# Hybrid attention and SSD layer: V's DRAM copies, convolution tiles and split-weight stores issued by GpSimd, output weights split in 20 products, one pair more from raw weights

## The chip, the core and the metric

The kernel runs on one core of a Trainium2 chip. The core has five engines that run side by side, each through its own list of instructions in order: TensorE (PE; its weight loads are shown as PEld), VectorE (DVE), ScalarE (ACT), GpSimd (POOL) and SyncE (SP), which only issues transfers (DMAs). ScalarE and GpSimd issue transfers too, from the same list as their arithmetic. The metric is the time of one execution in microseconds (us) on the device, the median of 3 runs; less is better.

## The reference

One decoder layer on x (2048 tokens, 1024 wide, float32). An input projection of 6672 columns feeds two branches, attention over three dilations and a Mamba-2 state-space mixer; both are gated and normed, joined and projected back. Cut to what matters here:

```python
proj = jnp.einsum('bsd,de->bse', x, w_in[layer])
q, k, v, z_att, z_ssm, xbc, dt_raw = jnp.split(proj, list(SPLITS), axis=-1)
o1, l1 = dilated_window_attention(q, k, v, slopes, 1)
o2, l2 = dilated_window_attention(q, k, v, slopes, 4)
o3, l3 = dilated_window_attention(q, k, v, slopes, 16)
wts = jax.nn.softmax(jnp.stack([l1, l2, l3], axis=0), axis=0)
y_att = wts[0][..., None] * o1 + wts[1][..., None] * o2 + wts[2][..., None] * o3
y_att = rms_norm(y_att.reshape(Bsz, S, D_ATT) * jax.nn.silu(z_att), att_norm_g[layer])
xbc = jax.nn.silu(causal_depthwise_conv(xbc, conv_w[layer], conv_b[layer]))
xs, bm, cm = jnp.split(xbc, [...], axis=-1)
...
y = ssd_chunked(xs_h, dt, a, bm, cm) + d_skip[layer][:, None] * xs_h
y_ssm = rms_norm(y.reshape(Bsz, S, D_SSM) * jax.nn.silu(z_ssm), ssm_norm_g[layer])
mix = jnp.concatenate([y_att, y_ssm], axis=-1)
out = jnp.einsum('bse,ed->bsd', mix, w_out[layer])
x = layer_norm(alpha * x + out, ln_g[layer], ln_b[layer])
```

## The kernel before

Every float32 operand of a large product is held as a high and a low part (h and l in the tile names), and a product is three matmuls: high x high, high x low, low x high.

**Stages.** (1) To 211 us: V and dt are projected; x is split, and parts and half-sums of x are stored to DRAM (d_T) for the next stage. The first eight row blocks of the output weights are scaled, split and stored to d_wo here (`split_w`). A scheduler orders this stage. (2) To 1279 us: 44 **jobs**, each of two 128-column blocks times one half of the tokens (1024). A job is a Strassen-like scheme of seven products in the order B11, T1, B21, T2, B22, T4, T3 (`products`); a product is 12 matmuls of 128 x 512. The token side of the half lies in 14 tiles (TB11h, TB11l, TT1h, ... of 128 x 2048, 1 MB each), loaded from d_T by GpSimd (L229, `token_side`) when the half changes: before job 0, during job 9 for job 10, during job 31 for job 32. The column side is four blocks of raw weights per job: ScalarE issues the loads `wr<-w` (L240) two jobs ahead, VectorE forms sums (L254), ScalarE casts the high part (L261), GpSimd subtracts for the low part (L262), giving seven tiles w. ScalarE (L315) or VectorE (L321, L323) moves each product out of PSUM, and TensorE needs the bank again three products later. (3) To about 1800 us: attention. (4) To the end: the output projection.

**Jobs.** Jobs 0 to 9 are the convolution ("c") and SSM gate ("s") columns of the first half; 10 to 31 the second half with all columns; 32 to 43 q, k and z of the first half. For jobs 32 to 43 the four weight tiles that are sums were saved to d_wc by SyncE when they were made for the second half (L264), and are reloaded by GpSimd (L282, `column_reload`); the other three are made anew from raw weights (L285, L286). From job 22 on the chunk steps of the state-space mixer (`ssd1` to `ssd6`) run between the products.

**What sets the order.** In stage 2 the order is written by hand: after each product `flush` runs what stands in `later` for this product's number (seven per job), and `after(n, f)` puts f n products later. So each engine's list is fixed, and a transfer waits in the list of the engine that issues it. Side work that hangs on the numbers:

- `copy_v`: 32 copies of V within DRAM, 512 KB each, in the two orders that the dilations 4 and 16 need, issued by ScalarE (L492), one every four products from product 3 on (jobs 0 to 18).
- `wout_load` and `split_w`: the other eight row blocks of the output weights, as 16 halves: load by ScalarE (L652), three products later the split by ScalarE (L117) and VectorE (L118), and at once the store by SyncE (L119); halves are loaded from product 36 to 61.
- `conv_tile`: the tile U of a convolution block, 128 x 19 x 128. Three transfers by SyncE (L391 twice in 512-byte rows, L392) bring the first half's results from d_cu, where job 0 to 9 put them (L385); the second half's products are added beside them, then ScalarE and VectorE run the four taps over U (L409, L412), ScalarE the SiLU (L418), and SyncE stores it (L424, L427). There are two U buffers.
- `sums_load`, `sums_part`: the half-sums of x; those of the first half are made in stage 1, those of the second in jobs 1 to 4 (L100, L108 to L112).
- SyncE also stores every finished column block (d_za, d_qh, ... L354, L365, L366, L377).

Of the kernel before, what the change touches and what calls it, by code (L numbers as in the profile page):

```python
# [9 lines left out]
F32 = mybir.dt.float32  # L10
# [7 lines left out]
D = 1024  # L18
# [10 lines left out]
def hybrid_layer(ctx, tc, xT, xc, w52, wv, convw, convb, dtb, alog, dskp, gcol, wout,  # L29
# [56 lines left out]
    with ExitStack() as c1:  # L86
# [25 lines left out]
            nc.sync.dma_start(dap(d_T[p, nm], k * 512, [[2048, 128], [128 * 2048, 2], [1, 512]]), t.bitcast(F32))  # L112


        def split_w(e, hf, raw, t):
            g = gc[:, e:e + 1]
            nc.scalar.activation(t[:, 0], raw, AF.Copy, scale=g)  # L117
            nc.vector.scalar_tensor_tensor(t[:, 1], raw, g, t[:, 0].bitcast(F32), op0=OP.mult, op1=OP.subtract)  # L118
            nc.sync.dma_start(d_wo[e][:, :, hf * 512:hf * 512 + 512], t.bitcast(F32))  # L119


        with tc.tile_pool(name="ts", bufs=1, reuse_waits="tile") as ts, \
# [57 lines left out]
            for pc in range(4):  # L180
                for i in range(2):
                    pst = [pp.tile([128, 512], F32, name="pp") for _ in range(5)]
                    pst += [ss.tile([128, 512], F32, name="ss") for _ in range(3)]
                    for k in range(8):
                        if i == 0:
                            load_v(pc, k)
                        if pc == 0:
                            load_x(k, i)
                        for r in range(8):
                            v_mm(pst[r], pc, 8 * i + r, k)  # L190
                    for r in range(8):
                        v_out(pst[r], pc, 8 * i + r)
                if pc == 0:
                    nc.sync.dma_start(ident, cst[:, 0:128])
                    nc.sync.dma_start(tri, cst[:, 128:256])
                    nc.sync.dma_start(cw, convw)
                    nc.sync.dma_start(cb, convb)
                    nc.sync.dma_start(dsk, dskp)
                    nc.sync.dma_start(gc, gcol)
                if pc < 2:  # L200
                    for k in (2 * pc, 2 * pc + 1):
                        r = sums_load(ts, 0, k)
                        for c in range(4):
                            sums_part(ts, 0, k, r, c)
                if pc in (1, 2):
                    quarters(pc - 1)
                if pc > 1:
                    for e in range(4 * pc - 8, 4 * pc - 4):
                        raw = ts.tile([128, 1024], F32, name="st", bufs=4)
                        nc.sync.dma_start(raw, wout[e * 128:(e + 1) * 128])  # L210
                        for hf in range(2):
                            split_w(e, hf, raw[:, 512 * hf:512 * hf + 512],
                                    ts.tile([128, 2, 512], F32R, name="to", bufs=6))
# [174 lines left out]
        def conv_tile(i, U):  # L388
            u = cp.tile([128, 19, NJ], F32, name="U", bufs=2)
            for tb in range(2):  # L390
                nc.sync.dma_start(u[:, 3 + tb:19:4, :], d_cu[i][:, tb].rearrange("p (s j) -> p s j", j=NJ))  # L391
            nc.sync.dma_start(u[:, 0, 1:NJ], d_cu[i][:, 1, 3 * NJ:4 * NJ - 1])  # L392
            nc.gpsimd.memset(u[:, 0:3, 0:1], 0.0)
            U.append(u)

# [93 lines left out]
        def copy_v(d, b):  # L489

            o = (b % 4 * 512 + b // 4 * 32, 8 * b)[d - 1]
            nc.scalar.dma_start(d_v[d][b], dap(d_v[0], o * D, [[128 * D, (4, 16)[d - 1]], [D, (32, 8)[d - 1]], [1, D]]))  # L492


        b64 = lambda a, n, g: a[:, n, 8 * g:8 * g + 8][:, :, None].to_broadcast([128, 8, 64])
# [150 lines left out]
        with tc.manual_schedule(engines={E.PE, E.DVE, E.Activation, E.Pool}):  # L646
# [3 lines left out]
            def wout_load(j):  # L650
                raw = sums.tile([128, 512], F32, name="woraw", bufs=3)
                nc.scalar.dma_start(raw, wout[j // 2 * 128:j // 2 * 128 + 128, j % 2 * 512:j % 2 * 512 + 512])  # L652
                after(3, lambda: split_w(j // 2, j % 2, raw, sums.tile([128, 2, 512], F32R, name="wot", bufs=4)))
            for j in range(16):
                later.setdefault(7 * 5 + 1 + 5 * j // 3, []).append(lambda j=j: wout_load(16 + j))
            for j in range(32):
                later.setdefault(4 * j + 3, []).append(lambda j=j: copy_v(1 + j // 16, j % 16))
            sums = sub.enter_context(tc.tile_pool(name="sums", bufs=1, side="right", reuse_waits="tile"))
            raws = {0: sums_load(sums, 1, 0)}
            for m, (ph, (kind, i)) in enumerate(jobs):  # L660
                p = ph % 2
                nT = T
                if m + 1 < len(jobs):
                    ph2 = jobs[m + 1][0]
                    if ph2 == 2:
                        nW, prep = column_reload(m + 1 - 32, q)
                    else:
                        u = [x for _, x in jobs[32:]].index(jobs[m + 1][1]) if jobs[m + 1][1] in rest else None
                        nW, prep = column_side(q, u)
                    for j, f in enumerate(prep):  # L670
                        after(j, f)
# [2 lines left out]
                        for j in range(7):  # L674
                            after(j, steps[j])
                if m + 2 < len(jobs):
                    q2, steps_ = column_load(*cts[m + 2], nc.scalar, jobs[m + 2][0] == 2)
                    for n, f in zip((3, 4, 6, 7), steps_):
                        after(n, f)
                if 10 < m + 1 < len(jobs) and jobs[m + 1][1][0] == "c":  # L680
                    Un = [None]
                    after(5, lambda i=jobs[m + 1][1][1], U=Un: (U.clear(), conv_tile(i, U)))
                to = None
                if kind == "c" and p == 0:
                    fin = fin_u(i)
                elif kind == "c":
                    U, U2 = U2 or [], None
                    if not U:
                        after(0, lambda i=i, U=U: conv_tile(i, U))
                    after(3, lambda i=i, U=U: conv_tile(i + 1, U))  # L690
                    to = lambda ci, q, U=U: U[ci][:, 5 + q:19:4, :]
                    fin = conv_fin(i, U)
                elif kind == "s":
# [552 lines left out]
```

## Time and profile before

| | us |
|---|---|
| median of 3 runs | 2204.65 (2201.44 to 2204.94) |
| profiled execution | 2207.89 |
| its span, first to last instruction | 2206.1 |
| TensorE busy in it | 2058.6 (93%) |
| ScalarE, VectorE, GpSimd busy | 1153.3, 1375.1, 1047.0 |

| stretch | length us | TensorE busy us | mean DMA share |
|---|---|---|---|
| V projection, 0 to 211.2 | 211.2 | 191.6 | 0.96 |
| jobs 0 to 22, 211.2 to 725.5 | 514.3 | 464.4 | 0.75 |
| jobs with chunk steps, to 1279 | 553.5 | 525.2 | 0.88 |
| attention, to 1800 | 521.0 | 507.3 | 0.70 |
| output, to 2206.1 | 406.1 | 370.1 | 0.39 |

How to read it: the profile is one execution. Busy time counts arithmetic; an engine that waits to issue a transfer counts as idle. In the lists of waits and in timelines, `<-` behind an idle time names what ended it, an instruction or the landing of a transfer (`DMA out<-in`). ACTq and SPq are the issuing of transfers by ScalarE and SyncE. Some matmul records can be missing from a trace.

### The profile page before, as it was taken

To read this page: it belongs to the slowest core of one execution; us is meant where nothing else is said; L and a number is where in the kernel's file an instruction comes from. 1 tells how busy PE (TensorE), PEld (TensorE's weight loads), DVE (VectorE), ACT (ScalarE), POOL (GpSimd) and SP (SyncE) were. 2 spreads that over 40 slices of the span, in tenths; PEclk is the share of its full clock that TensorE was granted. 3 is DMA by queue.
4 is the path that set the end of the run, shared out by engine and by line. 5 is a ranking of instruction groups with operands and counts; after the bars stand their busy time and mean duration, and the time that the engine had idled before them with its cause. 6 is when DMAs were issued, how large, how long until landed. Compare 5 with 4: busy or idle time off the path is not lost.

```text
span 2206.1 us, 38841 instructions
## 1 busy us (share of the span) xinstructions
PE 2058.6 (93%) x13824; PEld 1712.9 (78%) x13824; DVE 1375.1 (62%) x3141; ACT 1153.3 (52%) x3003; POOL 1047.0 (47%) x815
## 2 busy tenths in 40 slices
PE   8999899869999999979999999999999986999998
PEld 7998777648887787857888878888788865888886
DVE  3431554328899677735555548888888855655655
ACT  3231444326555676645666558888888841222221
POOL 2123434436776576744555422766666671322322
PEclk9999989979999999989999979999999988999999
DMA  9999677886767888898889853778777799332220
GB/s 328 370 327 337 219 264 243 298 327 183 243 208 265 306 308 305 299 400 276 283 263 291 279 208 115 218 220 241 222 195 207 209 366 271 107 107 83 86 90 29
DMA packets 275377, 529.19 MB, mean 240 GB/s; under 512 B 44784, under 2 KB 136048, under 8 KB 259184
## 3 DMA queue, kind: packets, MB, share of 16 engines
q1 hardware_dynamic: 201312, 272.93, 38.9%
q0 software_dynamic: 29968, 154.15, 19.6%
q10 hardware_dynamic: 43904, 99.64, 13.7%
q8 instruction: 109, 1.79, 0.3%
q14 instruction: 84, 0.69, 0.1%
HBM read 347.98 MB, written 195.43 MB: 246 GB/s over the span
## 4 chain that ended last, share of the span: by engine, by line
PE 49%; DMA 14%; DVE 7%; ACT 5%; issue 4%; POOL 3%; ACTq 1%; SPq 0%; DVEq 0%; POOLq 0%
PE N L861 6%; PE S L812 6%; PE T L841 6%; PE pp L306 5%; PE pp L310 5%; PE pp L308 5%; PE S L1021 3%; PE S L1023 3%; PE S L1022 3%; PE T L1021 2%; PE T L1022 2%; PE T L1023 2%; DVE acc L412 2%; DMA U<-d_cu 2%; DMA zt<-d_zs 2%
## 5 line engine op out<-in xcount | busy, mean ns | idle before, releaser
L262 POOL TENSOR_TENSOR w<-wr,w 128x512 fp32r<-128x512 f32 x224 | 357.0, 1614 | 226.3 <-ACT w L261 192.8
L828 ACT ACTIVATE P<-P,st 128x256 f32<-128x256 f32 (+1 forms) x768 | 345.2, 451 | 98.0 <-DVE st L820 97.5
L820 DVE CUSTOM_DVE_ANT_0 P<-S,tb 128x256 f32<-128x256 f32 (+1 forms) x768 | 235.1, 362 | 83.7 <-PE S L812 46.3
L315 ACT COPY ev<-pp 128x512 f32<-128x512 f32 x176 | 102.3, 581 | 208.1 <-PE pp L310 121.0
L843 DVE COPY PT<-T 128x512 f32<-128x512 f32 (+1 forms) x304 | 196.5, 677 | 1.4 <-PE T L841 1.4
L841 PE MATMUL T<-ident,P 128*128 128x128 f32 x1200 | 178.8, 286 | 5.9 <-DVE PT L843 5.9
L861 PE MATMUL N<-PT,v 128*64 128x128 f32 x2400 | 176.4, 284 | 1.0 <-DMA v<-d_v 1.0
L261 ACT CAST w<-wr 128x512 fp32r<-128x512 f32 x224 | 133.7, 618 | 75.8 <-DVE wr L254 36.7
L254 DVE TENSOR_TENSOR wr<-wr 128x512 f32<-128x512 f32 x128 | 129.2, 1010 | 66.6 <-DMA wr<-w 62.4
L861 PEld LDWEIGHTS N<-PT,v 128*64 128x64 f32 x2400 | 129.2, 138 | 34.2 <-issue 22.6
L841 PEld LDWEIGHTS T<-ident,P 128*128 128x128 f32 x1200 | 129.8, 142 | 30.2 <-DVE PT L843 7.2
L828 ACT ACTIVATION_READ_ACCUMULATOR P<-P,st 128x1 f32 x768 | 143.8, 187 | 0.0
L928 POOL TENSOR_TENSOR wb<-num,wb 128x2048 f32<-128x2048 f32 x21 | 96.3, 4588 | 98.5 <-ACT P L828 71.1
L323 DVE TENSOR_TENSOR ev<-pp,ev 128x512 f32<-128x512 f32 x152 | 100.6, 682 | 51.8 <-PE pp L310 39.6
L812 PE MATMUL S<-kh,qp 64*128 64x256 f32 (+1 forms) x1024 | 126.5, 306 | 0.0
L998 DVE TENSOR_REDUCE tb<-P 128x128 f32<-128x1024 f32 x32 | 63.9, 1998 | 84.4 <-PE N L1027 49.2
L363 DVE SCALAR_TENSOR_TENSOR ev<-ev 128x512 f32<-128x512 f32 x64 | 66.6, 1054 | 64.1 <-ACT ev L362 64.0
L812 PEld LDWEIGHTS S<-kh,qp 64*128 64x128 f32 x1024 | 88.9, 188 | 22.0 <-issue 20.7
L146 PE MATMUL pp<-vh,xh 128*128 128x256 f32 (+1 forms) x320 | 90.4, 289 | 15.8 <-ACT xh L169 15.8
L412 DVE SCALAR_TENSOR_TENSOR acc<-U,cw,acc 128x2048 f32<-128x2048 f32 x36 | 101.3, 2813 | 3.1 <-ACT acc L409 2.6
L139 POOL TENSOR_TENSOR vl<-vraw,vh 128x256 fp32r<-128x256 f32 (+1 forms) x32 | 30.0, 940 | 131.7 <-ACT vh L138 110.0
L147 PE MATMUL pp<-vl,xh 128*128 128x256 f32 (+1 forms) x320 | 90.8, 288 | 0.0
(364 smaller groups left out, 6037.3 us busy)
## 6 DMA issues: line engine op xcount, KB each, us to landing
wr<-w ACTq DMA_DIRECT2D x156, 256.0 KB
d_wc<-w SPq DMA_DIRECT2D x48, 512.0 KB
w<-d_wc POOLq DMA_DIRECT2D x48, 512.0 KB, 6.7
v<-d_v POOLq DMA_DIRECT2D x24, 1024.0 KB, 6.9
wb<-d_wd SPq DMA_DIRECT2D x48, 512.0 KB
csb<-d_cs ACTq DMA_DIRECT2D x32, 512.0 KB
st<-xT SPq DMA_DIRECT2D x31, 512.0 KB
d_v<-vt SPq DMA_DIRECT2D x16, 512.0 KB
```

The costliest lines, as they stand in the source:

```text
L254: tt = lambda o, a, b, op=OP.subtract: nc.vector.tensor_tensor(q[o], q[a], q[b], op=op)
L261: nc.scalar.copy(t[:, 0], q[nm])
L262: nc.gpsimd.tensor_tensor(t[:, 1], q[nm], t[:, 0].bitcast(F32), op=OP.subtract)
L306: nc.tensor.matmul(ps, w[:, 0, k], th[:, k], start=start and k == 0, stop=False, skip_group_check=not start)
L308: nc.tensor.matmul(ps, w[:, 0, k], tl[:, k], start=False, stop=False, skip_group_check=not start)
L412: return lambda: nc.vector.scalar_tensor_tensor(acc[0], U[:, j:j + 16, :], cw[:, i, j:j + 1], acc[0], op0=OP.mult, op1=OP.add)
L812: nc.tensor.matmul(ov(sp[h][:, 256 * b:256 * b + w]), A["q"][d][x][hr, blk], kv(A["k"][y][hr]), start=(m == 0), stop=(m == 2))
L820: nc.vector.tensor_tensor_reduce(P[:, h, b, 256 - w:256], sp[h][:, c0:c0 + w], tab[:, h, tab.shape[2] - w:], 1.0, 3.0e38, OP.add, OP.min, ...
L828: nc.scalar.activation(p, p, AF.Exp, bias=stat(A, 0, d, h, blk), scale=-1.0, accum_out=stat(A, 1, d, h, blk))
L841: nc.tensor.transpose(tp[:, h, b], P[:, h, b, 128 * which:128 * which + 128], ident)
L843: nc.vector.tensor_copy(pt[:, :, bl[0]:2], tp[:, :, bl[0]:2])
L861: nc.tensor.matmul(nm[64 * h:64 * h + 64, bq * 128:bq * 128 + 128], v[:, k, 64 * h:64 * h + 64], pts[which][:, h, b], start=(f or not whic ...
```

## The change

Five edits, all before stage 3:

- The copies of V (`copy_v`) are issued by GpSimd. The first 13 stay at their products; the other 19 come 22 products later (from product 77 in job 11 to product 149 in job 21), so that none falls between product 52 and product 76.
- `conv_tile` issues its three loads on GpSimd, one product later than before.
- The 16 stores of split output weights in stage 2 are issued by GpSimd two products after the split; the halves are loaded from product 35 to 55, about three every four products, 20 products in all.
- Job 32 (columns q of blocks 0 and 1, first half) makes all seven weight tiles from raw weights, as jobs 0 to 31 do. It loads four raw blocks instead of three, and its four sums are neither saved nor reloaded. Jobs 33 to 43 stay as they were.
- In stage 1 the half-sums of the first half are written one pass later in the code.

```diff
@@ -112,11 +112,15 @@
             nc.sync.dma_start(dap(d_T[p, nm], k * 512, [[2048, 128], [128 * 2048, 2], [1, 512]]), t.bitcast(F32))
 
 
-        def split_w(e, hf, raw, t):
+        def split_w(e, hf, raw, t, store=True):
             g = gc[:, e:e + 1]
             nc.scalar.activation(t[:, 0], raw, AF.Copy, scale=g)
             nc.vector.scalar_tensor_tensor(t[:, 1], raw, g, t[:, 0].bitcast(F32), op0=OP.mult, op1=OP.subtract)
-            nc.sync.dma_start(d_wo[e][:, :, hf * 512:hf * 512 + 512], t.bitcast(F32))
+            put_w = lambda queue: queue.dma_start(d_wo[e][:, :, hf * 512:hf * 512 + 512], t.bitcast(F32))
+            if store:
+                put_w(nc.sync)
+            else:
+                after(2, lambda: put_w(nc.gpsimd))
 
 
         with tc.tile_pool(name="ts", bufs=1, reuse_waits="tile") as ts, \
@@ -197,8 +201,8 @@
                     nc.sync.dma_start(cb, convb)
                     nc.sync.dma_start(dsk, dskp)
                     nc.sync.dma_start(gc, gcol)
-                if pc < 2:
-                    for k in (2 * pc, 2 * pc + 1):
+                if 0 < pc < 3:
+                    for k in (2 * pc - 2, 2 * pc - 1):
                         r = sums_load(ts, 0, k)
                         for c in range(4):
                             sums_part(ts, 0, k, r, c)
@@ -388,8 +392,8 @@
         def conv_tile(i, U):
             u = cp.tile([128, 19, NJ], F32, name="U", bufs=2)
             for tb in range(2):
-                nc.sync.dma_start(u[:, 3 + tb:19:4, :], d_cu[i][:, tb].rearrange("p (s j) -> p s j", j=NJ))
-            nc.sync.dma_start(u[:, 0, 1:NJ], d_cu[i][:, 1, 3 * NJ:4 * NJ - 1])
+                nc.gpsimd.dma_start(u[:, 3 + tb:19:4, :], d_cu[i][:, tb].rearrange("p (s j) -> p s j", j=NJ))
+            nc.gpsimd.dma_start(u[:, 0, 1:NJ], d_cu[i][:, 1, 3 * NJ:4 * NJ - 1])
             nc.gpsimd.memset(u[:, 0:3, 0:1], 0.0)
             U.append(u)
 
@@ -489,7 +493,7 @@
         def copy_v(d, b):
 
             o = (b % 4 * 512 + b // 4 * 32, 8 * b)[d - 1]
-            nc.scalar.dma_start(d_v[d][b], dap(d_v[0], o * D, [[128 * D, (4, 16)[d - 1]], [D, (32, 8)[d - 1]], [1, D]]))
+            nc.gpsimd.dma_start(d_v[d][b], dap(d_v[0], o * D, [[128 * D, (4, 16)[d - 1]], [D, (32, 8)[d - 1]], [1, D]]))
 
 
         b64 = lambda a, n, g: a[:, n, 8 * g:8 * g + 8][:, :, None].to_broadcast([128, 8, 64])
@@ -650,11 +654,11 @@
             def wout_load(j):
                 raw = sums.tile([128, 512], F32, name="woraw", bufs=3)
                 nc.scalar.dma_start(raw, wout[j // 2 * 128:j // 2 * 128 + 128, j % 2 * 512:j % 2 * 512 + 512])
-                after(3, lambda: split_w(j // 2, j % 2, raw, sums.tile([128, 2, 512], F32R, name="wot", bufs=4)))
+                after(3, lambda: split_w(j // 2, j % 2, raw, sums.tile([128, 2, 512], F32R, name="wot", bufs=4), False))
             for j in range(16):
-                later.setdefault(7 * 5 + 1 + 5 * j // 3, []).append(lambda j=j: wout_load(16 + j))
+                later.setdefault(35 + 4 * j // 3, []).append(lambda j=j: wout_load(16 + j))
             for j in range(32):
-                later.setdefault(4 * j + 3, []).append(lambda j=j: copy_v(1 + j // 16, j % 16))
+                later.setdefault(4 * j + (3 if j < 13 else 25), []).append(lambda j=j: copy_v(1 + j // 16, j % 16))
             sums = sub.enter_context(tc.tile_pool(name="sums", bufs=1, side="right", reuse_waits="tile"))
             raws = {0: sums_load(sums, 1, 0)}
             for m, (ph, (kind, i)) in enumerate(jobs):
@@ -662,10 +666,10 @@
                 nT = T
                 if m + 1 < len(jobs):
                     ph2 = jobs[m + 1][0]
-                    if ph2 == 2:
+                    if ph2 == 2 and ph2 == ph:
                         nW, prep = column_reload(m + 1 - 32, q)
                     else:
-                        u = [x for _, x in jobs[32:]].index(jobs[m + 1][1]) if jobs[m + 1][1] in rest else None
+                        u = rest.index(jobs[m + 1][1]) if ph2 == 1 and jobs[m + 1][1] in rest[1:] else None
                         nW, prep = column_side(q, u)
                     for j, f in enumerate(prep):
                         after(j, f)
@@ -674,12 +678,12 @@
                         for j in range(7):
                             after(j, steps[j])
                 if m + 2 < len(jobs):
-                    q2, steps_ = column_load(*cts[m + 2], nc.scalar, jobs[m + 2][0] == 2)
+                    q2, steps_ = column_load(*cts[m + 2], nc.scalar, m + 2 > 32)
                     for n, f in zip((3, 4, 6, 7), steps_):
                         after(n, f)
                 if 10 < m + 1 < len(jobs) and jobs[m + 1][1][0] == "c":
                     Un = [None]
-                    after(5, lambda i=jobs[m + 1][1][1], U=Un: (U.clear(), conv_tile(i, U)))
+                    after(6, lambda i=jobs[m + 1][1][1], U=Un: (U.clear(), conv_tile(i, U)))
                 to = None
                 if kind == "c" and p == 0:
                     fin = fin_u(i)
@@ -687,7 +691,7 @@
                     U, U2 = U2 or [], None
                     if not U:
                         after(0, lambda i=i, U=U: conv_tile(i, U))
-                    after(3, lambda i=i, U=U: conv_tile(i + 1, U))
+                    after(4, lambda i=i, U=U: conv_tile(i + 1, U))
                     to = lambda ci, q, U=U: U[ci][:, 5 + q:19:4, :]
                     fin = conv_fin(i, U)
                 elif kind == "s":
```

In the rows below, line numbers of the changed kernel are its own, four higher from L119 on (L315 is L319, L262 is L266, and so on).

ScalarE's list in job 10, from the first copy out of PSUM on. Before:

```order
L315 COPY ev<-pp 128x512
L261 CAST w<-wr 128x512
L240 DMA wr<-w 128x512
L315 COPY ev<-pp 128x512
L492 DMA d_v_102<-d_v_100 16x8192
L261 CAST w<-wr 128x512 x3
L315 COPY ev<-pp 128x512
L261 CAST w<-wr 128x512
L240 DMA wr<-w 128x512 x2
L315 COPY ev<-pp 128x512
L492 DMA d_v_102<-d_v_100 16x8192
```

In the changed kernel, at the same four copies:

```order
L319 COPY ev<-pp 128x512
L265 CAST w<-wr 128x512
L244 DMA wr<-w 128x512
L319 COPY ev<-pp 128x512
L265 CAST w<-wr 128x512 x3
L319 COPY ev<-pp 128x512
L265 CAST w<-wr 128x512
L244 DMA wr<-w 128x512 x2
L319 COPY ev<-pp 128x512
```

The copies of V are gone from between the PSUM copies; the weight loads (`wr<-w`) stay where they were.

GpSimd's list at the end of the T loads of the second half, jobs 9 and 10 (`w<-wr,w` is the low part of a weight tile). Before:

```order
L229 DMA TT3h<-d_T1T_121 128x2048
L229 DMA TT3l<-d_T1T_121 128x2048
L262 TENSOR_TENSOR w<-wr,w 128x512
L393 MEMSET U 128x3
L262 TENSOR_TENSOR w<-wr,w 128x512 x4
L393 MEMSET U 128x3
L262 TENSOR_TENSOR w<-wr,w 128x512 x8
```

In the changed kernel:

```order
L233 DMA TT3h<-d_T1T_121 128x2048
L233 DMA TT3l<-d_T1T_121 128x2048
L266 TENSOR_TENSOR w<-wr,w 128x512
L395 DMA U<-d_cu_123 128x4x128 x2
L396 DMA U<-d_cu_123 128x127
L397 MEMSET U 128x3
L266 TENSOR_TENSOR w<-wr,w 128x512 x4
L395 DMA U<-d_cu_124 128x4x128 x2
L396 DMA U<-d_cu_124 128x127
L397 MEMSET U 128x3
L266 TENSOR_TENSOR w<-wr,w 128x512 x2
L496 DMA d_v_101<-d_v_100 4x2x16384
```

The loads of the first two U tiles now stand behind the last T loads, each in front of its memset and of the weight tiles that follow; a copy of V stands five rows on.

GpSimd's list at the T loads of the third part, jobs 31 and 32, with state updates of the chunk steps between (H, xd). Before:

```order
L229 DMA TT2h<-d_T0T_113 128x2048
L229 DMA TT2l<-d_T0T_113 128x2048
L282 DMA w<-d_wc 128x1024
L229 DMA TB22h<-d_T0B_111 128x2048
L229 DMA TB22l<-d_T0B_111 128x2048
L562 TENSOR_TENSOR H_6209<-H_6209,dec 128x512
L572 TENSOR_TENSOR xd<-xd,y 128x512
L282 DMA w<-d_wc 128x1024
L229 DMA TT4h<-d_T0T_115 128x2048
L229 DMA TT4l<-d_T0T_115 128x2048
```

In the changed kernel:

```order
L233 DMA TT2h<-d_T0T_113 128x2048
L233 DMA TT2l<-d_T0T_113 128x2048
L233 DMA TB22h<-d_T0B_111 128x2048
L233 DMA TB22l<-d_T0B_111 128x2048
L566 TENSOR_TENSOR H_6205<-H_6205,dec 128x512
L576 TENSOR_TENSOR xd<-xd,y 128x512
L266 TENSOR_TENSOR w<-wr,w 128x512
L233 DMA TT4h<-d_T0T_115 128x2048
L233 DMA TT4l<-d_T0T_115 128x2048
```

The reloads of w between the T loads are gone, and one L266 stands in the place of each a little further on.

In stage 1 all engines have the same rows in the same order as before, and TensorE's list is the same throughout.

## Prediction

> **What bounds the kernel now.** First the slices of the page: TensorE is busy nearly everywhere, and its clock drops only where it pauses.
>
> ```profile
> PE   8999899869999999979999999999999986999998
> PEclk9999989979999999989999979999999988999999
> ```
>
> The gaps that the change can reach lie between 211 and 1260 us, in the 44 projection jobs. I cut that stretch at job starts (the first matmul on tile TB11h of a job in TensorE's timeline): jobs 0 to 2, 3 to 6, 7 and 8, 9, 10, 11 to 17, 18 to 22, 23 to 31, 32, 33 to 42.
>
> ```profile
> core 0: us, PE busy (x) PEld busy (x) DVE busy (x) ACT busy (x) POOL busy (x), PEclk, DMA share, GB/s
> 211.20:284.10 72.90, 63.81 (x257) 51.70 (x257) 42.95 (x67) 31.29 (x54) 34.93 (x31) 0.88 0.71 233
> 284.10:368.90 84.80, 80.71 (x340) 65.43 (x339) 38.85 (x55) 38.31 (x67) 38.15 (x28) 0.96 0.74 250
> 368.90:412.50 43.60, 39.02 (x169) 31.31 (x169) 17.45 (x22) 17.59 (x32) 18.31 (x13) 1.00 0.78 278
> 412.50:440.00 27.50, 20.99 (x86) 16.63 (x84) 7.75 (x12) 8.53 (x15) 12.51 (x13) 0.88 0.86 306
> 440.00:490.30 50.30, 28.90 (x85) 21.23 (x86) 9.84 (x15) 9.40 (x15) 15.90 (x19) 0.73 0.96 357
> 490.30:623.60 133.30, 133.30 (x590) 110.42 (x589) 119.93 (x90) 76.63 (x123) 93.97 (x53) 1.00 0.63 194
> 623.60:725.50 101.90, 97.71 (x422) 79.80 (x421) 93.54 (x73) 59.20 (x94) 69.13 (x40) 0.98 0.79 261
> 725.50:952.20 226.70, 218.34 (x1183) 180.12 (x1182) 161.74 (x239) 158.60 (x320) 152.54 (x118) 1.00 0.88 310
> 952.20:1004.30 52.10, 33.44 (x127) 25.60 (x126) 13.28 (x24) 18.23 (x38) 20.63 (x23) 0.74 1.06 401
> 1004.30:1260.10 255.80, 254.52 (x1440) 211.87 (x1439) 144.69 (x257) 166.06 (x339) 133.97 (x132) 1.00 0.85 274
> ```
>
> Jobs 11 to 17 never let TensorE wait: 133.3 / 7 = 19.04 us is the clean job, 2.72 us per product. Against it jobs 3 to 6 are 8.6 us over, 7 and 8 together 5.5, 9 is 8.5, **10 is 31.3**, 18 to 22 are 6.7. Jobs 33 to 42 carry chunk units and take 25.6 each; against these **job 32 is 26.5 over**. The clock is granted at 0.73 and 0.74 in jobs 10 and 32, so a pause costs more than its own length.
>
> Next, what job 10 waits for, in TensorE's timeline (start, length, instruction, idle time before it and what ended it):
>
> ```profile
> 443.19 0.50 PE L308 MATMUL pp<-TB11l,w 128*128 128x512 f32 x1 [2.74 <-DMA TB11l<-d_T1B]
> 451.62 0.80 PE L308 MATMUL pp<-TT1l,w 128*128 128x512 f32 x1 [3.82 <-DMA TT1l<-d_T1T]
> 459.00 0.50 PE L308 MATMUL pp<-TB21l,w 128*128 128x512 f32 x1 [1.89 <-DMA TB21l<-d_T1B]
> 464.51 0.79 PE L308 MATMUL pp<-TT2l,w 128*128 128x512 f32 x1 [2.19 <-DMA TT2l<-d_T1T]
> 479.50 0.80 PE L306 MATMUL pp<-TB22h,w 128*128 128x512 f32 x1 [10.71 <-ACT ev L315]
> ```
>
> Two causes: the token-side tiles T of the second half arrive late, then ScalarE's copy out of PSUM is late. ScalarE's and SyncE's timelines tell why:
>
> ```profile
> 451.56 0.62 ACT L261 CAST w<-wr 128x512 fp32r<-128x512 f32 x1
> 478.48 0.34 ACTq L240 DMA_DIRECT2D wr<-w  x1
> 478.86 0.58 ACT L315 COPY ev<-pp 128x512 f32<-128x512 f32 x1 [26.68 <-DMA U<-d_cu]
> 443.21 1.66 SPq L391 DMA_DIRECT2D U<-d_cu  x2
> 454.90 13.32 SPq L391 DMA_DIRECT2D U<-d_cu  x2
> 468.26 9.61 SPq L392 DMA_DIRECT2D U<-d_cu  x1
> ```
>
> ScalarE stands at a 256 KB weight load that cannot be issued before a convolution-tile load of SyncE has landed: the transfers of both engines share a few completion slots. For 26.68 us no copy leaves PSUM. Jobs 7 and 9 show the same with other transfers in front:
>
> ```profile
> 378.08 0.62 ACT L261 CAST w<-wr 128x512 fp32r<-128x512 f32 x1 [6.85 <-DMA d_cu<-ev]
> 413.04 0.62 ACT L261 CAST w<-wr 128x512 fp32r<-128x512 f32 x1 [6.93 <-DMA woraw<-wout]
> 424.83 0.62 ACT L261 CAST w<-wr 128x512 fp32r<-128x512 f32 x1 [9.36 <-DMA d_cu<-ev]
> 429.71 0.55 POOL L229 DMA_DIRECT2D TB11h<-d_T1B  x1
> ```
>
> The last row is a consequence: the first T load of the second half is issued 17.2 us after job 9 began, because GpSimd stood in front of it waiting for ScalarE's casts.
>
> **The change part by part.** *Copies, tile loads and stores off the shared slots* (32 + 36 + 16 transfers). (a) Job 9 then runs its clean 19.04 us from 412.5. TB11h may be issued when product 0 is done (2.7 us) and one L262 (1.3) has passed, at 416.5 in place of 429.7. In the rows above the four pairs of T had landed 13.5, 21.9, 29.3 and 34.8 us after that issue; the other three follow at the last pace, 5.5 us, the nearest row: 40.3, 45.8, 51.3. From 416.5 the last pair is there at 467.8, and job 10 ends one product later, 470.5 instead of 490.3: **-19.8**. At 5.5 us a pair throughout it would be -24.6, at the slower 7.4 of 451.62 to 459.00 it is -13.2. T is what ends last then; the copies are no longer late. The U loads now follow T on GpSimd's queue; L409 may wait a few us for them on ScalarE, under that same wait for T. (b) Jobs 7 and 8: 5.5 over, nearly all such slot waits: **-4.5** (0 to -5.5). (c) Jobs 3 to 6: 8.6 over. Part of it is ScalarE waiting for a store to land,
>
> ```profile
>   DMA d_T1T<-to: 10.5, 3
> 668.58 0.59 ACT L315 COPY ev<-pp 128x512 f32<-128x512 f32 x1 [2.35 <-DMA d_qh<-ev]
> 674.07 0.63 ACT L362 ACTIVATE ev<-ev 128x512 fp32r<-128x512 f32 x1 [2.39 <-DMA d_qh<-ev]
> ```
>
> and the V copies still move the same bytes: I take half, **-4** (0 to -8.6). (d) Jobs 18 to 22: the other two rows are stores that SyncE issues late, behind U loads and weight saves; 12 loads of these jobs and four saves leave its queue: **-3** (0 to -6.7).
>
> *GpSimd's side.* No row shows a DRAM copy, a store or a 512-row load issued there. The nearest are its loads of 128 rows (TB11h), 256 (d_uh) and 2048 (v):
>
> ```profile
> L229 POOL DMA_DIRECT2D TB11h<-d_T0B x2: 554/574/594, 171.5 to 935.7; - x2
> L973 POOL DMA_DIRECT2D num<-d_uh x6: 703/713/759, 1791.0 to 1823.1; - x6
> L756 POOL DMA_DIRECT2D v<-d_v x24: 1148/1190/1239, 1282.0 to 1745.2; - x24
> L262 POOL TENSOR_TENSOR w<-wr,w x80: 1270/1638/3390, 480.2 to 696.7; 128x512 fp32r<-128x512 f32 x80
> L412 DVE SCALAR_TENSOR_TENSOR acc<-U,cw,acc 128x2048 f32<-128x2048 f32 x36 | 101.3, 2813 | 3.1 <-ACT acc L409 2.6
> POOL U L393 <- DMA d_xs<-U: 23.5, 8, 4.5
> ```
>
> I take 0.72 us an issue (ends 0.55 and 1.24). The tight place is jobs 11 to 17, where GpSimd is busy 93.97 of 133.3 us: three U issues a job and a copy every four products make 33 issues, 24 us (18 to 41). 118 of 133 still fits, and a weight half is finished several products before its use. The U loads must wait for the old tile's store, but GpSimd waits for it already at the memset (23.5 us in all), and the loads stand one product later. I put **+1** (0 to +3). In jobs 5 to 8 the 16 stores and the copies add some 4 us a job to the 9 that jobs 7 and 8 show; hidden. The quickened weight splits (20 products) move ScalarE and VectorE work within jobs where both are under half busy: 0.
>
> The trace has one warning: beside the convolution taps of L412 an L262 takes up to 3390 ns instead of 1270. The Trainium skill ("DMA: Bandwidth & Descriptors", section SWDGE vs HWDGE vs iDMA) says that GpSimd writes its transfer descriptors into SBUF, from which VectorE shuts it out in its two-port modes, and that transfers issued by SyncE and ScalarE are immune; that speaks against this change. Here L756 stays at 1148 to 1239 ns beside a busy VectorE, but no issue of this trace lies beside L412, so the rule is a rival below.
>
> *One pair more from raw weights.* Job 32's four combined weight tiles are no longer reloaded between the T loads.
>
> ```profile
> w<-d_wc POOLq DMA_DIRECT2D x48, 512.0 KB, 6.7
> wr<-w ACTq DMA_DIRECT2D x156, 256.0 KB
> ```
>
> Job 32 runs its transfers at a share of 1.06 and 401 GB/s, full. Four times 512 KB go, one 256 KB load comes: 1.8 MB / 401 GB/s = **-4.6** (0, if what TensorE waits for is elsewhere; -12, about half the overrun, if the waits of GpSimd for its own slots shorten too). The four casts and L262 that come instead (0.6 and 1.3 us each) fall in job 31, where ScalarE and GpSimd are 70% busy: hidden; without that cover 5 us. The four saves gone are in (d).
>
> *The half-sum loads one pass later in stage 1*: every engine's rows stand in the same order there, so 0; its 20 us of TensorE gaps bound it both ways, but nothing moves.
>
> **Sum**: -19.8 - 4.5 - 4 - 3 + 1 - 4.6 = -34.9. The profiled execution took 2207.9 us (span 2206.1 and 1.8 around it): 2173.0. The median of the runs is 3.2 us below that execution, so I predict **2170**.
>
> **Rivals.** *Only the names of the waits change* (17%): ScalarE still issues the weight loads and shares slots with d_cu stores and woraw loads, which stand in the rows of jobs 7 and 9 as the transfers waited for. For it: removing V, U and d_wo leaves these. Against: SyncE issued those d_cu stores late because it stood at d_wo and U. If job 9 still loses its 8.5, T starts no earlier, and job 10 saves only its 10.71 us copy wait: 2204.65 - 12 = **2193**.
>
> *GpSimd becomes the bound in jobs 11 to 20* (9%, ends slower). L412 fills 101.3 us of the 235 from 490.3 to 725.5, 43%. If an issue that meets a tap waits out the train of three (8.4 us, 4.2 on average), 33 issues cost 33 x (0.72 + 0.43 x 4.2) = 83 us, GpSimd needs 177 of 133, and TensorE loses 6.3 us a job, 63 over ten jobs: 2170 + 63 = **2233**. It decides from a mean issue of 2.0 us: then the loss of ten jobs, (33 x 2.0 + 94 - 133) / 0.7 = 38, has eaten the gain. The highest issue seen, 1.24 us, speaks against it. By the Trainium skill's rule above, an issue beside a two-port instruction would be held like this.
>
> *More than forecast* (7%): the overruns of jobs 3 to 8 and 18 to 22 go wholly, T lands at the faster pace, job 32 saves 12: -57, **2147**. *The change does nothing that counts* (3%), the time goes into other waits for T: **2205**.
>
> **How the numbers follow.** Forecast 64%, its own range 2152 to 2188 (job 10's ends, and half of the others). With the 2193 case's near side and the 2147 case I give 2147 to 2194; outside are the far side of the first rival and the slower ones. A measurement here tells 0.2%, 4.4 us, from no change: faster 0.87, same 0.05, slower 0.08.
>
> **What would show it.** Right: no wait of ScalarE on U, d_v or d_wo; TB11h of the second half issued about 4 us after job 9 starts; job 9 near 19 us, job 10 near 39 with waits on T alone; jobs 11 to 17 still 19.04; job 32 near 47. Wrong: issues of L395 or L496 beyond 2 us beside the taps; TensorE waiting for GpSimd's weight halves in jobs 11 to 20; T pairs landing slower than 7.4 us apart.

## The result, and the profile after

| | before | changed | ratio, 95% interval |
|---|---|---|---|
| first measurement, 3 runs each | 2204.65 | 2182.01 (2171.41 to 2183.47) | 0.9887 (0.9848 to 0.9926) |
| measured again | 2206.67 | 2180.17 (2176.99 to 2182.72) | 0.9882 (0.9868 to 0.9896) |

The changed kernel is faster by 1.2%, some 25 us; 2170 was predicted. The profiled execution took 2171.41 us (span 2169.6), the fastest of its three, so its 36.5 us against the profile of before are 10 to 14 more than the medians differ by (22.6 and 26.5).

The page's slices of the changed kernel, TensorE busy and its clock:

```profile
PE   7999998989999999979999999999999977999998
PEclk9999999989999999999999979999999988999999
```

The windows of the changed kernel, cut at the same job starts as before (jobs 0 to 2, 3 to 6, 7 and 8, 9, 10, 11 to 17, 18 to 22, 23 to 31, 32):

```profile
core 0: us, PE busy (x) PEld busy (x) DVE busy (x) ACT busy (x) POOL busy (x), PEclk, DMA share, GB/s
209.40:279.30 69.90, 61.83 (x257) 50.17 (x257) 43.10 (x66) 30.72 (x54) 37.75 (x36) 0.93 0.74 240
279.30:362.80 83.50, 79.18 (x341) 64.29 (x339) 46.81 (x58) 39.41 (x69) 42.07 (x38) 0.98 0.77 264
362.80:409.80 47.00, 40.31 (x169) 32.57 (x168) 27.31 (x28) 21.39 (x38) 27.50 (x29) 0.93 0.84 288
409.80:428.90 19.10, 19.10 (x86) 15.80 (x85) 7.71 (x9) 7.10 (x13) 15.54 (x18) 1.00 1.04 373
428.90:466.70 37.80, 26.44 (x86) 18.92 (x85) 5.61 (x10) 7.59 (x12) 15.28 (x19) 0.82 1.01 379
466.70:601.00 134.30, 133.96 (x590) 110.12 (x588) 122.39 (x89) 76.18 (x123) 107.64 (x84) 1.00 0.63 193
601.00:706.40 105.40, 99.56 (x422) 80.52 (x421) 95.76 (x74) 58.24 (x92) 79.23 (x59) 0.97 0.82 270
706.40:929.90 223.50, 218.17 (x1183) 180.17 (x1182) 161.96 (x238) 159.19 (x321) 154.69 (x120) 1.00 0.87 310
929.90:974.80 44.90, 29.01 (x126) 21.89 (x125) 14.84 (x27) 18.72 (x40) 19.72 (x20) 0.89 1.02 389
```

Job 9 is clean (27.5 to 19.1) and job 10 went from 50.3 to 37.8, job 32 from 52.1 to 44.9. But jobs 7 and 8 are **longer** (43.6 to 47.0), and so are jobs 18 to 22 (101.9 to 105.4), against the forecast.

TensorE's and GpSimd's timelines of the changed kernel at job 10 answer to those of before:

```profile
433.42 0.50 PE L312 MATMUL pp<-TT1l,w 128*128 128x512 f32 x1 [1.45 <-DMA TT1l<-d_T1T]
441.01 0.80 PE L312 MATMUL pp<-TB21l,w 128*128 128x512 f32 x1 [3.25 <-DMA TB21l<-d_T1B]
451.09 0.50 PE L312 MATMUL pp<-TB22l,w 128*128 128x512 f32 x1 [1.94 <-DMA TB22l<-d_T1B]
462.54 0.80 PE L312 MATMUL pp<-TT3l,w 128*128 128x512 f32 x1 [2.04 <-DMA TT3l<-d_T1T]
```

```profile
415.21 0.57 POOL L233 DMA_DIRECT2D TB11h<-d_T1B  x1
```

The first T load leaves 5.4 us after job 9 began, not 17.2, and job 10 waits for T alone. ScalarE's list of waits from 211 to 760 us has these rows where before it had 26.7 us for U in front of a copy out of PSUM:

```profile
ACT wot L117 <- DMA d_wo<-wot: 5.3, 2, 3.7
ACT acc L413 <- DMA U<-d_cu: 3.7, 1, 3.7
ACT w L265 <- DMA d_zs<-ez: 3.1, 1, 3.1
```

The first is a new wait: a split of the output weights finds its buffer not yet stored.

What GpSimd paid for an issue stands in the views of lines L395, L396, L496 and L119 (min/median/max in ns):

```profile
L395 POOL DMA_DIRECT2D U<-d_cu x24: 747/768/808, 443.8 to 664.3; - x24
L396 POOL DMA_DIRECT2D U<-d_cu x12: 547/550/564, 448.8 to 665.1; - x12
L496 POOL DMA_DIRECT2D d_v<-d_v x32: 514/572/835, 224.2 to 676.8; - x32
L119 POOL DMA_DIRECT2D d_wo<-wot x16: 677/695/822, 348.7 to 409.0; - x16
```

0.72 us was assumed. No issue takes over 0.84 us, though 24 of L395's and L396's 36 and 11 of L496's 32 overlap a convolution tap in the trace.

### The profile page after: what moved, and what is told of

Same layout as the page of the kernel before. It is cut to its first block, busy times and chain, and to the rows that moved or that the text cites. A ratio compares the mean times of both kernels' runs of the same rounds, so it can differ in the third digit from the quotient of the medians.

```text
span 2169.6 us, 38851 instructions
## 1 busy us (share of the span) xinstructions
PE 2048.0 (94%) x13824; PEld 1703.7 (79%) x13824; DVE 1394.1 (64%) x3145; ACT 1154.4 (53%) x3007; POOL 1092.5 (50%) x899
## 4 chain that ended last, share of the span: by engine, by line
PE 47%; DMA 8%; DVE 5%; ACT 3%; issue 3%; POOL 2%; ACTq 0%; SPq 0%; POOLq 0%; DVEq 0%
PE S L816 7%; PE N L865 7%; PE T L845 6%; PE S L1025 4%; PE S L1027 3%; PE S L1026 3%; PE pp L310 3%; PE pp L314 3%; PE pp L312 3%; PE T L1025 2%; PE T L1026 2%; PE T L1027 2%; DMA TT3l<-d_T0T 1%; DVE P L824 1%; ACT P L832 1%
## 5 line engine op out<-in xcount | busy, mean ns | idle before, releaser
L266 POOL TENSOR_TENSOR w<-wr,w 128x512 fp32r<-128x512 f32 x231 | 357.2, 1562 | 177.5 <-ACT w L265 146.5
L319 ACT COPY ev<-pp 128x512 f32<-128x512 f32 x176 | 102.2, 581 | 184.9 <-PE pp L314 123.4
L865 PEld LDWEIGHTS N<-PT,v 128*64 128x64 f32 x2400 | 129.2, 138 | 33.2 <-issue 22.6
L258 DVE TENSOR_TENSOR wr<-wr 128x512 f32<-128x512 f32 x132 | 145.0, 1099 | 15.6 <-DMA wr<-w 12.5
L416 DVE SCALAR_TENSOR_TENSOR acc<-U,cw,acc 128x2048 f32<-128x2048 f32 x36 | 105.2, 2922 | 3.2 <-ACT acc L413 2.8
L367 DVE SCALAR_TENSOR_TENSOR ev<-ev 128x512 f32<-128x512 f32 x64 | 64.2, 1015 | 64.3 <-ACT ev L366 64.2
L143 POOL TENSOR_TENSOR vl<-vraw,vh 128x256 fp32r<-128x256 f32 (+1 forms) x32 | 29.7, 933 | 130.5 <-ACT vh L142 125.7
L1064 POOL TENSOR_TENSOR kh<-kh,wb 128x1024 f32<-128x1024 f32 x8 | 19.2, 2398 | 142.6 <-DVE kh L1063 142.6
```

What stands on the lines that cost most here:

```text
L258: tt = lambda o, a, b, op=OP.subtract: nc.vector.tensor_tensor(q[o], q[a], q[b], op=op)
L266: nc.gpsimd.tensor_tensor(t[:, 1], q[nm], t[:, 0].bitcast(F32), op=OP.subtract)
L865: nc.tensor.matmul(nm[64 * h:64 * h + 64, bq * 128:bq * 128 + 128], v[:, k, 64 * h:64 * h + 64], pts[which][:, h, b], start=(f or not whic ...
```

## The experiments

All runs together, the times of jobs from TensorE's timeline of each profile. The last column but two adds up VectorE's 36 convolution taps (L412, in the changed kernel L416), the next gives the longest of them. Each profile is one execution, while the ratio is taken from all runs: the profile of the raw pair undone lies 10.3 us below its median, that of the d_wo pace undone 10.2 above.

| kernel | jobs 3-8 | 9+10 | 11-22 | 32 | taps | longest | ratio to before |
|---|---|---|---|---|---|---|---|
| before | 128.4 | 77.8 | 235.2 | 52.1 | 101.3 | 3.46 | 1 |
| changed | 130.5 | 56.8 | 239.7 | 44.9 | 105.2 | 3.48 | 0.9887 |
| changed, again | 130.9 | 54.7 | 242.1 | 42.7 | 111.1 | 9.83 | 0.9882 |
| U on SyncE | 131.0 | 58.8 | 245.7 | 45.1 | 113.9 | 9.82 | 0.9909 (0.9894 to 0.9924) |
| V on ScalarE | 135.2 | 55.6 | 246.7 | 43.0 | 110.5 | 9.82 | 0.9953 (0.9939 to 0.9968) |
| d_wo part undone | 121.8 | 57.0 | 240.5 | 42.5 | 105.6 | 3.48 | **0.9857** (0.9840 to 0.9873) |
| raw pair undone | 131.8 | 55.9 | 239.7 | 52.4 | 105.4 | 3.48 | 0.9913 (0.9892 to 0.9935) |
| V's places undone | 129.6 | 62.5 | 239.3 | 44.5 | 110.4 | 6.90 | 0.9905 (0.9892 to 0.9918) |
| V wholly undone | 137.4 | 70.2 | 241.1 | 45.7 | 113.2 | 9.83 | 1.0003 (0.9990 to 1.0017) |
| before + V's places | 126.5 | 64.9 | 244.2 | 53.4 | 101.8 | 3.46 | 0.9984 (0.9974 to 0.9993) |
| before + V part | 125.1 | 63.4 | 253.0 | 53.4 | 120.5 | 9.99 | 0.9976 (0.9965 to 0.9986) |
| d_wo pace undone | 121.7 | 64.2 | 241.7 | 42.9 | 110.7 | 10.06 | 0.9861 (0.9840 to 0.9882) |
| five split buffers | 129.9 | 55.6 | 239.6 | 43.1 | 105.9 | 3.48 | 0.9873 (0.9853 to 0.9892) |
| V placed anew | 116.9 | 56.2 | 257.4 | 42.9 | 117.3 | 9.95 | 0.9884 (0.9866 to 0.9903) |

### One part undone at a time

**U on SyncE.** `nc.gpsimd.dma_start(u...)` to `nc.sync.dma_start(u...)` in all three loads.

> The changed kernel with one part undone: the three loads of a convolution tile U are issued by SyncE again (still one product later than in the kernel before). Theory A (the prediction's: the U loads on SyncE, and what stands behind them, kept ScalarE's weight loads waiting): job 10 again has a late copy out of PSUM of about 10 us after T has landed, and d_cu stores may be late again; jobs 9 and 10 together 66 to 78 us in place of 56.8, the median 10 to 20 us above the changed kernel's 2182, so 2192 to 2202. Theory B (the earlier end of the output-weight loads, product 55 in place of 61, is what freed job 9, and T's earlier start gave job 10): job 9 stays at 19.04, the two jobs grow by less than 6 us, the median 2182 to 2188.

2187.11 us. Job 9 stays clean and jobs 9 and 10 grow by 2 to 4: theory A falls there. (Theory B's figures come out; its cause is tested two runs on.) ScalarE's timeline of this kernel shows why that cost so little:

```profile
448.95 0.59 ACT L319 COPY ev<-pp 128x512 f32<-128x512 f32 x1 [15.45 <-DMA U<-d_cu]
```

The wait for U is back, but TensorE's idle time in this job ends only on T's landings: the stall hides under them. What is lost lies in jobs 11 to 22 instead (4 to 6 us).

**V on ScalarE.** `nc.gpsimd.dma_start(d_v[d][b]...)` to `nc.scalar.dma_start(...)`, places as changed.

> The changed kernel with one part undone: the 32 copies of V are issued by ScalarE again, at the changed products (none between products 52 and 76). Theory A: jobs 9 and 10 keep their 56.8 us, since no copy stands there; jobs 2 to 7 lose some us, and jobs 11 to 21 lose little, since their slots are free; 0 to 8 us, median 2182 to 2190. Theory C (GpSimd's own load by the copies is what costs in jobs 11 to 22, and the shared slots do not matter): jobs 11 to 22 become faster by 2 to 8 us, median 2174 to 2182.

2195.03 us, 15 above the changed kernel: the largest single loss, twice what theory A allowed, and jobs 9 and 10 have no share in it (55.6). It is spread: 3.6 us in jobs 0 to 2, 4 to 5 in 3 to 8, 5 to 7 in 11 to 22. Theory C falls.

**The output-weight part.**

```diff
-later.setdefault(35 + 4 * j // 3, []).append(lambda j=j: wout_load(16 + j))
+later.setdefault(7 * 5 + 1 + 5 * j // 3, []).append(lambda j=j: wout_load(16 + j))
-after(3, lambda: split_w(..., False))
+after(3, lambda: split_w(...))
```

> The changed kernel with one part undone: the split output weights are stored by SyncE at once, and their loads run from product 36 to 61 again. Theory A: job 7 gets rid of the wait of ScalarE for its own d_wo stores (the split tile has 4 buffers, the store two products later: 3.7 and 1.5 us seen before L117), so jobs 6 to 7 become 3 to 6 us shorter, and jobs 8 and 9 stay within 3 us, since the U loads and copies of V are still away: median 2176 to 2184. Theory B (the pace of these loads freed job 9): job 9 goes back to 24 to 27 us and job 10's T loads start that much later, 8 to 16 us in all: median 2188 to 2196.

2173.82 us: **faster than the changed kernel** by the medians, though the intervals of the two ratios still touch (0.9840 to 0.9873 against 0.9868 to 0.9896), with 9 us less in jobs 3 to 8 and nothing lost in 9 and 10. Theory B falls; this part of the change costs.

**The raw pair.** Job 32 reloads its four sums from d_wc again, and they are saved.

> The changed kernel with one part undone: job 32 reloads its four combined weight tiles from d_wc again, and they are saved. Theory A: job 32 takes 50 to 53 us in place of 44.9, all else within 2 us, median 2187 to 2190. Rival (job 32 is set by the landing of T alone, and its 7.2 us came from T's loads starting at another time): job 32 stays at 45 to 47, median 2182 to 2184.

2189.48 us; job 32 at 52.4, all other stretches within 2 us. Theory A holds: the gain of job 32 is the raw pair's.

### What freed job 9

None of the undoings brought job 9's loss back, so the copies' places (the gap from product 52 to 76) and their queue were taken apart. The changed kernel was timed again beside them:

> The changed kernel itself, unedited, timed once more beside the kernel before in the same call as the three below. All theories: 2180 to 2184 median; the first profile (2171.4) was 11 us below the other two executions, and if that was the length of the half-clock stretch where attention starts (27.3 us there), this profile shows jobs 0 to 43 within 3 us of the first one (1039 us from job 0 to 43) and the difference behind them.

2180.17 us, as expected, but not for the reason given. Against the first profile (span 2180.7 to 2169.6), 3.9 us lie from job 43 on; 6.0 lie in the jobs before it, among them 2.4 in 11 to 22 and 5.6 in 23 to 31, less 2.1 in 9 and 10 and 2.2 in 32. A single profile of this kernel is good for 2 to 6 us in such a stretch, no better.

**V's places undone, queue kept:** `4 * j + (3 if j < 13 else 25)` to `4 * j + 3`.

> The changed kernel with the copies of V still issued by GpSimd, but all at the old places, one every four products from product 3 to 127. Theory D (the gap between products 52 and 76, in which no copy stands, is what freed job 9 and lets T land early): copies lie between and beside the T loads again, T's pairs land 1 to 3 us further apart, jobs 9 and 10 take 62 to 72 us in place of 56.8, median 2188 to 2198. Theory E (what freed job 9 is that ScalarE no longer issues copies, wherever they stand): jobs 9 and 10 stay at 56 to 60, median 2180 to 2186, and jobs 11 to 21 become 1 to 4 us shorter.

2185.02 us; jobs 9 and 10 take 62.5: TB11h leaves 9.1 us after job 9's start, the last T load 40.0 in place of 30 to 31. The jobs go as theory D has it, the median 3 us less far.

**V wholly undone:** `4 * j + 3`, on ScalarE, the rest of the change in place.

> The changed kernel with the copies of V wholly as before: issued by ScalarE, one every four products from product 3 to 127; all other parts of the change stay. Theories D and E, which both put job 9 down to the copies: job 9 takes 24 to 28 us, job 10 40 to 50, together 64 to 78 in place of 56.8, and jobs 2 to 8 lose 5 to 9; median 2195 to 2205. Theory F (several parts of the change each suffice to free job 9): the two jobs stay within 4 us of 56.8, median 2184 to 2192.

2206.87 us, **no gain left** (1.0003). Job 9 loses 5.9, TB11h leaves 15.8 us after its start, jobs 9 and 10 take 70.2, jobs 3 to 8 take 137.4. Of the whole time, undoing the queue alone cost 15 us, the places alone 5, both 27. Theory F falls.

**The kernel before with the new places alone:**

> The kernel before with one part of the change alone: the copies of V stay on ScalarE, but those from the 14th on come 22 products later, so that none stands between products 52 and 76. Theory D: job 9 near 19 to 21, job 10 about 40 to 48 (the late copy behind the U loads stays, but lies mostly under T's landing), together 60 to 68 in place of 77.8, median 8 to 16 us below the kernel before. Theories E and F: job 9 still loses 4 us or more (d_cu stores late behind SyncE's d_wo stores and U loads), together 70 to 78, median within 6 us of the kernel before.

Job 9 at 19.0, and 64.9 with job 10, as theory D has it. But the time is only 3 us below the kernel before, not the 8 to 16 of theory D: jobs 11 to 22, which now hold the copies on ScalarE's queue, take 9 more and jobs 23 to 31 four.

### Why jobs 7 and 8 grew

**Pace alone undone** (loads from product 36 to 61, stores on GpSimd two products later), and **five split buffers** (`name="wot", bufs=5`, pace as changed):

> The changed kernel with the output-weight loads at the pace of before (products 36 to 61); the stores stay on GpSimd, two products after the split. Jobs 7 and 8 took 47 us in the changed kernel and 40.7 with pace and stores both undone. Theory R (the ring of four split buffers: at one half per 1.33 products a buffer is wanted again after 5.3 products = 14.5 us, while its store is issued 5.4 us after the split and takes 6.5 to 10.6 us to land, so ScalarE waits at L117, 5.3 to 6.9 us in the profiles): at the old pace a buffer is wanted after 18 us, no wait of L117 for d_wo, jobs 7 and 8 take 41 to 43, median 2173 to 2178. Theory S (what cost is that the stores stand on GpSimd's queue): jobs 7 and 8 stay at 45 to 48, median 2179 to 2184.

> The changed kernel with five buffers for the split output weights in place of four, pace and stores as changed. Theory R: a buffer is wanted again after 6.7 products = 18 us, so the waits of L117 for d_wo go, jobs 7 and 8 take 41 to 44, median 2174 to 2179. Theory S, or a theory P (the quicker pace itself costs, by more work and transfers a product): jobs 7 and 8 stay at 45 to 48, median 2179 to 2184; P differs from S by the run with the old pace.

At the old pace jobs 7 and 8 are clean, in the windows of that kernel:

```profile
362.90:401.10 38.20, 38.20 (x170) 31.44 (x169) 17.83 (x23) 19.09 (x34) 22.76 (x23) 1.00 0.84 300
```

The stores stand on GpSimd there, so theory S falls. With five buffers jobs 7 and 8 still take 47.0, so theory R falls as well. Rows of ScalarE's timelines at product T2 of job 7, first of the changed kernel, then with five buffers:

```profile
370.26 0.72 ACT L117 ACTIVATE wot<-woraw,gc 128x512 fp32r<-128x512 f32 x1 [3.73 <-DMA d_wo<-wot]
374.10 0.62 ACT L265 CAST w<-wr 128x512 fp32r<-128x512 f32 x1 [3.13 <-DMA d_zs<-ez]
376.39 0.57 ACT L319 COPY ev<-pp 128x512 f32<-128x512 f32 x1
```

```profile
369.79 0.72 ACT L117 ACTIVATE wot<-woraw,gc 128x512 fp32r<-128x512 f32 x1 [4.38 <-DMA woraw<-wout]
372.83 0.62 ACT L265 CAST w<-wr 128x512 fp32r<-128x512 f32 x1 [2.32 <-DVE ev L327]
372.85 2.63 ACTq L244 DMA_DIRECT2D wr<-w  x1
376.21 0.56 ACT L319 COPY ev<-pp 128x512 f32<-128x512 f32 x1
```

The wait for the buffer is gone, and the copy out of PSUM that TensorE waits for still leaves at 376.2: the raw half itself now lands late (4.38 us), and the issue of the weight load behind it takes 2.63. It is the pace (theory P): three halves in four products put their loads and splits into the list that copies PSUM faster than the transfers come.

The old pace with stores on GpSimd has a price of its own: its last stores fall among the T loads (TB11h 9.3 us after job 9's start, one L119 standing between TT2l and TB22h), and jobs 9 and 10 take 64.2 in this one profile. That is what the quick pace is good for. With the stores on SyncE, neither price is paid in full (jobs 7 and 8 40.7, jobs 9 and 10 57.0). The medians do not tell the two versions apart: 2174.51 with the pace alone undone, 2173.82 with the whole part undone.

### Does V add up, and can it be better

> The kernel before with the V part of the change alone: copies on GpSimd, the last 19 of them 22 products later. The undoings give for the others: raw pair about -9, U loads about -7, output weights about +6. Theory G (the parts add up, with V's own share the largest): job 9 at 19, job 10 at 38 to 42, job 32 at 52 to 54, time 13 to 19 us below the kernel before, 2188 to 2194. Theory F (V alone does little without the others, as V's undoing alone took all of the gain): within 8 us of the kernel before, job 10 above 44.

2201.89 us, 5 below the kernel before: theory G's sum is 8 to 14 us too high, and theory F's figures come out (within 8 us, job 10 at 44.4). Job 9 is clean, job 10 not; ScalarE's and TensorE's timelines of this kernel show U in front again, this time beyond T's landing:

```profile
455.75 0.58 ACT L315 COPY ev<-pp 128x512 f32<-128x512 f32 x1 [28.32 <-DMA U<-d_cu]
```

```profile
456.39 0.80 PE L306 MATMUL pp<-TB22h,w 128*128 128x512 f32 x1 [13.46 <-ACT ev L315]
```

And jobs 11 to 22 take 253.0, 18 more than before. Three taps took 9.8 to 10.0 us there. The last run puts more copies into those jobs:

```diff
-4 * j + (3 if j < 13 else 25)
+(28 + 4 * j if j < 6 else 77 + 3 * (j - 6))
```

> The changed kernel with the output-weight part undone (as the run that undid it) and the copies of V placed anew, on GpSimd: none before product 28, six every four products to 48, none to 76, the other 26 every three products from 77 to 152. Theory A (jobs 0 to 3 wait for half-sum stores that share the DMA engines with the copies): jobs 0 to 3 take 4 to 8 us less than 89.3 to 91, jobs 11 to 22 stay within 2 us, median 2166 to 2171, below both kernels. Rival (seven more copies in jobs 11 to 21 cost there what is saved before, by GpSimd and VectorE keeping each other out: one tap of L416 took 9.83 us in place of 2.35 to 3.48 in several profiles): jobs 11 to 22 4 us or more longer than 236 to 242, median 2172 to 2180.

2181.45 us, no better than the changed kernel and 8 above the version with the d_wo part undone on which it is built. Jobs 3 to 8 fall to 116.9 (jobs 0 to 2 do not move, 69.6), but jobs 11 to 22 take 257.4: the rival's case, with three taps of 6.5 to 10 us, though the median lies 1.5 above its range. The taps are not all of it: of the 6.6 us that TensorE waits in job 20, the longest of these (29.9), 4.4 are for copies which stood behind stores of d_qh and d_ql. How a tap gets that long shows in the profile of the changed kernel measured again, first VectorE, then GpSimd:

```profile
547.49 12.21 DVE L416 SCALAR_TENSOR_TENSOR acc<-U,cw,acc 128x2048 f32<-128x2048 f32 x2 [0.93 <-ACT acc L413]
559.89 2.35 DVE L416 SCALAR_TENSOR_TENSOR acc<-U,cw,acc 128x2048 f32<-128x2048 f32 x1
```

```profile
547.09 2.55 POOL L266 TENSOR_TENSOR w<-wr,w 128x512 fp32r<-128x512 f32 x2
549.58 0.53 POOL L496 DMA_DIRECT2D d_v<-d_v  x1
550.12 5.04 POOL L266 TENSOR_TENSOR w<-wr,w 128x512 fp32r<-128x512 f32 x4
```

A tap alone takes 2.35 us. This one (9.83 of the 12.21) began 0.4 us after a train of six subtractions and ended 2.2 us after the train did: VectorE waited for all six, while each of them ran in its undisturbed 1.3 us. ScalarE's SiLU then waits for the tap, and casts stand behind the SiLU; GpSimd's next subtraction waits for a cast and TensorE for the subtraction:

```profile
562.33 1.34 ACT L422 ACTIVATE U<-acc,cb 128x512 f32<-128x512 f32 x2 [7.12 <-DVE acc L416]
565.49 1.79 POOL L266 TENSOR_TENSOR w<-wr,w 128x512 fp32r<-128x512 f32 x1 [10.32 <-ACT w L265]
567.33 0.50 PE L314 MATMUL pp<-TT1h,w 128*128 128x512 f32 x1 [1.14 <-POOL w L266]
```

So the 7.5 us that this tap lost cost TensorE 1.1 us directly. In the kernel before with the V part, a tap of 9.78 us in job 13 is followed in the same way by 4.7 us of waits in job 14, which took 27.1.

## Why the prediction was right, and where not

**Jobs 9 and 10, -19.8:** measured -21.0 and -23.1. Size and chain hold: T is issued 5.4 us after job 9's start (forecast 4), T ends last, and U costs ScalarE 3.7 us under that wait. But the step credited the transfers' queues alone. The new places of V's copies without any new queue bring 12.9 of the 21 (77.8 to 64.9); the rest of the change without the new places brings 15.3 (62.5). So each by itself does most of it, and with the places as changed, V on ScalarE, U on SyncE or the d_wo part undone each leave 55.6 to 58.8. U's queue matters only where the stall outlasts T: 13.5 us in the kernel before with the V part.

**Jobs 7 and 8, -4.5, and "the quickened weight splits: 0":** measured +3.4 and +3.9; this is the step that failed. It took half-idle engines as cover. Idle time does not help an in-order list in which a split must wait for its load. Without the quick pace the term is -5.4 (38.2) with the stores on GpSimd and -2.9 (40.7) with them on SyncE, both within what was forecast.

**Jobs 3 to 6, -4:** -1.3. With the d_wo part undone it is -3.7, with its pace alone undone still -1.3. By these single profiles the stores on GpSimd's queue take the rest; in what way is open.

**Jobs 18 to 22, -3, and GpSimd's side, +1:** together -2 for jobs 11 to 22, measured +4.5 and +6.9. The issue cost was right (0.51 to 0.84 us), and GpSimd did not become the bound. What the sum lacked lies first in job 22, which took 27.4 and 26.1 in place of 21.2; jobs 18 to 21 became 2.7 and 2.5 shorter, near the forecast, and jobs 11 to 17 took 1.1 and 4.5 more. TensorE's waits in job 22 of the first profile are 4.96 us, in place of 1.87 before, all for copies out of PSUM, and these stood behind stores of d_kh and d_kl:

```profile
688.34 0.58 ACT L319 COPY ev<-pp 128x512 f32<-128x512 f32 x1 [4.52 <-DMA d_kh<-ev]
688.97 0.50 PE L310 MATMUL pp<-TT2h,w 128*128 128x512 f32 x1 [1.69 <-ACT ev L319]
694.63 0.58 ACT L319 COPY ev<-pp 128x512 f32<-128x512 f32 x1 [3.12 <-DMA d_kl<-ev]
695.27 0.79 PE L310 MATMUL pp<-TB22h,w 128*128 128x512 f32 x1 [3.27 <-ACT ev L319]
```

Which move causes that was not separated: with U on SyncE job 22 takes 23.1, with V's places alone 20.6, with V's part alone 28.5. VectorE's taps lost 4 and 10 us in the two profiles, a term at nothing in the sum, but how much of the loss in jobs 11 to 17 is theirs is not shown: V's places undone has the taps at 110.4 and jobs 11 to 22 at 239.3, the places alone have them at 101.8 and 244.2.

**Job 32, -4.6:** -7.2 and -9.4, confirmed by the run without it. The mechanism was right; the size left out the clock, granted at 0.89 in place of 0.74. By the windows, TensorE's time not busy in this job fell by 2.8 us (18.7 to 15.9) and its busy time by 4.4 (33.4 to 29.0).

**Stage 1, 0:** holds; job 0 starts between 208.7 and 210.6 us in all thirteen later profiles, also in the two built on the kernel before.

In all, 10.6 us were lost against the forecast in jobs 3 to 8 and 6.5 to 9 in 11 to 22, and 3 to 5 won in job 32 and 3 in jobs 0 to 2: the median came out 12 above the forecast, inside the range. That the first profile fell by 36.5, near the sum of 34.9, is luck: 5.7 us of it lie from job 43 on and 3.2 in jobs 23 to 31, where nothing was forecast and where the second profile has 1.8 less and 2.4 more than before. Of the signs, TB11h, job 9 and job 10 (37.8, waits on T alone) came; ScalarE's waits on U and d_wo stayed, at 3.7 and 5.3 us, and one T pair landed 7.6 us after the one before (433.42 to 441.01), just over the 7.4 that was to count against the forecast. *Only the names of the waits change* falls with job 9 at 19.0. *GpSimd becomes the bound* falls as it was put, an issue held by a tap; the contention it feared exists the other way round. The fastest version, 0.9857, is the change without its output-weight part; the one with only the pace undone, 0.9861, is as fast.

## What to carry to other kernels

Where several engines share transfer slots, look at large transfers twice: can their place move away from the loads that end last, and can their queue change? Here both moves of V's copies were worth 27 us with the rest of the change in place, and only 5 without it; the places alone were worth 5 and 3. Give side work no more pace than its own loads can land at, however idle the engine looks: in an in-order list its waits are everybody's. Before work is packed onto GpSimd beside VectorE's long instructions, look at the longest of those instructions, not their mean.

## What the hardware showed that was not expected

A VectorE tap that starts behind a GpSimd subtraction usually waits for that one alone (3.3 to 3.5 us in place of 2.35), and the next subtraction then waits for the tap (3.0 us in place of 1.3 at 689.57 in the changed kernel). By the Trainium skill ("SBUF — State Buffer", section Who interferes with whom) an instruction with two SBUF inputs and a GpSimd instruction that reads SBUF exclude each other, whichever starts first; the trace agrees with that. Not expected was that a tap can lose its turn to a whole train, 9.83 us for 2.35: taps over 5 us stand in 8 of the 14 profiles, and in none of the two whose GpSimd issues neither U nor copies of V. That these issues cause it was not isolated: four profiles with them have no such tap, the first of the changed kernel among them.
